# A small early write to the output by every DMA engine, in a batched matrix multiplication that is bound by its transfers

## The chip, the cores and the metric

The kernel runs on one core of one Trainium2 chip. The metric is the time of one execution on the device, in microseconds (us). Where a ratio of two kernels is given, it is the mean time of one kernel's fast runs over that of the other's fast runs of the same rounds, so it isn't quite the ratio of the medians quoted beside it.

## The reference

```python
batch, m, k, n = 16, 512, 512, 512          # float32
def reference(a, b):                        # a: (batch, m, k), b: (batch, n, k)
    return np.matmul(a, b.transpose(0, 2, 1))
```

a, b and out have 16.8 MB each, 50.3 MB in all, and each byte crosses the core's DMA engines once.

## The kernel before

Matrices are worked on in pairs: eight loads of 2 MB from a, eight from b, sixteen stores of 1 MB. VectorE casts to bf16, TensorE transposes and multiplies, VectorE and ScalarE empty PSUM. The first load of b goes through ScalarE's queue, all others through SyncE's; the first eight stores go through GpSimd's queue, the others through SyncE's. The parts that matter here:

```python
        def load(n, engine=nc.sync):
            u, slot = n // 2, n % NL                      # NL = 7 load buffers
            ...
            engine.dma_start(ld[:, slot], src).then_inc(s_ld[slot], 16)

        def store(n):
            engine = nc.gpsimd if n < STORES.count("S") else nc.sync
            engine.wait_ge(s_out, n + 1)
            engine.dma_start(
                out[n].rearrange("(p j) n -> p j n", j=J), ob[:, n % NO]
            ).then_inc(s_st[n], 16)                        # NO = 7 output buffers

        load(0)
        load(1, nc.scalar)
        for n in range(2, NL):
            load(n)
        # ... SyncE: further loads and the late stores ...

        n_st = n_of = 0
        nc.gpsimd.wait_ge(s_ld[0], 32)      # hold the stores until the eighth load has landed
        for what in STORES:                 # "SSSSOSOSOSSOOOOOO": S = store, O = wait for one to land
            ...
```

## Time and profile before

| | |
|---|---|
| time, median of the first three runs | 125.56 us (125.42 to 125.84) |
| span of the profiled run | 123.7 us |
| TensorE, ScalarE, VectorE busy | 73%, 55%, 55% of the span |
| DMA engines busy | nearly all of the span, about 430 GB/s while they are (407 over the whole span) |
| first packet, last landing | 1.93 us, 122.26 us |

How to read it: a busy share is an average over the span, so what counts is which row is full from end to end. Here that is the DMA row. The lines that show it stand in the prediction.

The table by stretches counts a packet's bytes where the packet starts; a packet of 16 KB on 16 engines is 0.26 MB per turn, so in a stretch of 4 us it is a few per cent off. The finer reading takes every packet of the trace, spreads its bytes over its own duration and asks how many microseconds a stretch lost against 430 GB/s. I call that its **deficit**.

### The profile page before, as it was taken

The numbers are of one execution on the slowest core, as the hardware profiler recorded it, in microseconds if no ns is written. First come the engines' busy times: TensorE is split into PE (matmuls) and PEld (weight loads), VectorE is DVE, ScalarE is ACT, GpSimd is POOL, SyncE is SP. The second block draws the span as 40 slices with busy tenths as digits, with TensorE's granted clock in tenths as the row PEclk, the third lists the DMA queues.
The fourth block names the chain that finished last, engine by engine and source line by source line (L and its number), as shares of the span: only waits on it lengthen the run. The fifth ranks groups of instructions, "written<-read, shape, count | busy, mean of one in ns | idle before, by whom it ended". The sixth has DMA issues, their size and how long they took to land. (4 is left out here: it accounts for less than half of the span.)

```text
span 123.7 us, 2364 instructions
## 1 busy us (share of the span) xinstructions
PE 90.8 (73%) x768; PEld 55.9 (45%) x768; DVE 68.1 (55%) x96; ACT 68.0 (55%) x130; POOL 5.2 (4%) x14
## 2 busy tenths in 40 slices
PE   0000189999999899989998999999899919995000
PEld 0000177447644754674476347645754528441000
DVE  0000698983895689289918974865957078400000
ACT  4000065478855956795589369765946069655000
POOL 2000000000000250001010110000000000000000
PEclk9999999999999999999999999999999986999955
DMA  4999999999999999999999999999999999999990
GB/s 148 413 435 429 429 429 424 429 424 435 435 424 424 429 392 363 445 416 424 453 405 437 443 408 443 424 424 458 397 445 427 408 429 427 429 427 429 424 387 8
DMA packets 4608, 50.33 MB, mean 407 GB/s; under 512 B 512, under 2 KB 512, under 8 KB 512
## 3 DMA queue, kind: packets, MB, share of 16 engines
q1 hardware_dynamic: 3312, 39.85, 76.2%
q0 software_dynamic: 1152, 8.39, 16.1%
q10 hardware_dynamic: 144, 2.10, 4.2%
HBM read 33.55 MB, written 16.78 MB: 407 GB/s over the span
## 5 line engine op out<-in xcount | busy, mean ns | idle before, releaser
L249 PE MATMUL ps<-tb,ta 128*128 128x512 bf16 x256 | 57.8, 379 | 0.5
L207 ACT COPY ob<-ps 128x512 f32 x64 | 34.4, 589 | 29.2 <-PE ps L249 21.3
L189 ACT COPY ta<-tp 128x512 bf16<-128x512 bf16 x64 | 32.9, 610 | 15.0 <-PE tp L230 15.0
L249 PEld LDWEIGHTS ps<-tb,ta 128*128 128x128 bf16 x256 | 24.1, 98 | 30.6 <-issue 4.0
L230 PE MATMUL tp<-ident,ha 128*128 128x128 bf16 x256 | 19.3, 228 | 18.1 <-PEq L135 18.1
L230 PEld LDWEIGHTS tp<-ident,ha 128*128 128x128 bf16 x256 | 16.3, 102 | 21.9 <-issue 20.1
L170 DVE COPY tb<-tp 128x1024 bf16<-128x1024 bf16 x32 | 21.2, 684 | 4.2 <-DVEq L135 4.2
L230 PE MATMUL tp<-ident,hb 128*128 128x128 bf16 x256 | 18.5, 230 | 3.4 <-PEq L135 3.4
L230 PEld LDWEIGHTS tp<-ident,hb 128*128 128x128 bf16 x256 | 16.3, 103 | 4.0 <-issue 4.0
L154 DVE CAST ha<-ld 128x1024 bf16 x8 | 5.5, 687 | 14.3 <-DVEq L135 14.3
L165 DVE COPY ha<-wa 128x2048 bf16<-128x2048 bf16 x8 | 5.5, 691 | 12.7 <-DVEq L135 12.7
L160 DVE CAST wa<-ld 128x2048 bf16 x8 | 9.8, 1220 | 0.0
L160 DVE CAST wb<-ld 128x2048 bf16 x8 | 9.7, 1217 | 0.0
L154 DVE CAST hb<-ld 128x1024 bf16 x8 | 5.5, 692 | 7.3 <-DVEq L135 7.3
L103 POOL DMA_DIRECT2D out_dram<-ob x8 | 4.5, 570 | 65.5 <-DMA ld<-in_b_dram 40.9
L169 DVE COPY hb<-wb 128x2048 bf16<-128x2048 bf16 x8 | 5.5, 685 | 0.1
L157 DVE CAST ha<-ld 128x1024 bf16 x8 | 5.5, 686 | 0.0
L157 DVE CAST hb<-ld 128x1024 bf16 x8 | 5.5, 686 | 0.0
L180 ACT ACT_TABLE_LOAD x1 | 1.3, 1283 | 1.5 <-SPq L43 1.5
L79 POOL TENSOR_SCALAR_AFFINE_SELECT ident<-ident 128x128 bf16<-128x128 bf16 x1 | 0.3, 283 | 0.2 <-POOL ident L77 0.2
L77 POOL MEMSET ident<- 128x128 bf16 x1 | 0.2, 204 | 0.5 <-SPq L43 0.5
L180 ACT COPY one<-const-float32-1.0 128x1 f32<-128x1 f32 x1 | 0.2, 192 | 0.0
(4 smaller groups left out, 0.4 us busy)
## 6 DMA issues: line engine op xcount, KB each, us to landing
ld<-in_a_dram SPq DMA_DIRECT2D x8, 2048.0 KB, 26.5
ld<-in_b_dram SPq DMA_DIRECT2D x7, 2048.0 KB, 29.6
out_dram<-ob POOLq DMA_DIRECT2D x8, 1024.0 KB, 28.9
out_dram<-ob SPq DMA_DIRECT2D x8, 1024.0 KB, 19.7
ld<-in_b_dram ACTq DMA_DIRECT2D x1, 2048.0 KB, 12.0
```

The lines of the kernel that those rows point to most:

```text
L103: engine.dma_start(out[n].rearrange("(p j) n -> p j n", j=J), ob[:, n % NO]).then_inc(s_st[n], 16)
L154: nc.vector.tensor_copy(out=h[:, :J, :], in_=src[:, :J, :HK]).then_inc(s_cd, 1)
L157: nc.vector.tensor_copy(out=h[:, J:, :], in_=src[:, J:, :HK]).then_inc(s_c, 1)
L160: nc.vector.tensor_copy(out=w[:], in_=src[:, :, HK:]).then_inc(s_w, 1)
L165: nc.vector.tensor_copy(out=ha[:], in_=wa[:]).then_inc(s_ca, 1)
L169: nc.vector.tensor_copy(out=hb[:], in_=wb[:]).then_inc(s_cb, 1)
L170: nc.vector.tensor_copy(out=tb[:, ko, :], in_=tp[:, 2 + ko % 2].rearrange("k j p -> k (j p)"),).then_inc(s_eb, 1)
L180: nc.scalar.copy(out=one[:], in_=nc.const_aps.tensor(1.0, (P, 1), f32))
L189: c = nc.scalar.copy(out=ta[:, ko, e * J * P:(e + 1) * J * P].rearrange("k (j p h) -> k j p h", j=J, h=2), in_=tp[:, ko % 2, :, e * HP:(e ...
L207: c = nc.scalar.copy(out=dst[:, j, :].rearrange("m (p j) -> m p j", j=2 * J), in_=ps[:, j, :].rearrange("m (j p) -> m p j", j=2 * J),)
L230: t = nc.tensor.transpose(tp[:, 2 * x + g, j, :], h[:, j, g * P:(g + 1) * P], ident[:])
L249: t = nc.tensor.matmul(ps[:, j, :], ta[:, ko, (e * J + j) * P:(e * J + j + 1) * P], tb[:, ko, :].rearrange("k (j p) -> k j p", j=2 * J)[:, ...
```

## The change

Nothing is removed. ScalarE's queue, behind the first load of b, writes one zero by each of the sixteen DMA engines into the first megabyte of out (a "touch"), and GpSimd waits for this ahead of its first store, which later writes the right numbers there. The intent, as far as the edit shows it: let what the first write into out costs be paid early.

```diff
+        s_touch = sem("s_touch")
 ...
         load(0)
         load(1, nc.scalar)
+
+        nc.scalar.dma_start(
+            out[0].rearrange("(i r) n -> i r n", i=16)[:, 0, :1],
+            nc.const_aps.tensor(0.0, (16, 1), f32),
+            allow_slow_non_contiguous=True,
+        ).then_inc(s_touch, 16)
         for n in range(2, NL):
             load(n)
 ...
         n_st = n_of = 0
+        nc.gpsimd.wait_ge(s_touch, 16)
         nc.gpsimd.wait_ge(s_ld[0], 32)
```

## The prediction

> **What bounds the kernel now.** I read the forty-slice view first, then the chain that ended last, then a table of busy time by stretches, then the waits, and last the transfers one by one (start, length, size and queue of each packet, and the moment of each landing).
>
> The page's slices:
>
> ```profile
> PE   0000189999999899989998999999899919995000
> ...
> DMA  4999999999999999999999999999999999999990
> GB/s 148 413 435 429 429 429 424 429 424 435 435 424 424 429 392 363 445 416 424 453 405 437 443 408 443 424 424 458 397 445 427 408 429 427 429 427 429 424 387 8
> DMA packets 4608, 50.33 MB, mean 407 GB/s; under 512 B 512, under 2 KB 512, under 8 KB 512
> ```
>
> A slice is 123.7 / 40 = 3.09 us. The DMA row shows 9 from the second slice to the last but one, so the sixteen engines never rest. TensorE, at 73% of the span, starts in the fifth slice and is done before the stores are. The chain that ended last agrees in an indirect way: it stops at ScalarE's last copy, at 113.08 us, and accounts for only some 10% of the span. What lies after it is stores draining. The last store was issued at 113.7 us, its packets ended at 121.8 us and it landed at 122.26 us, so at the end the engines still had 8 us of queued work that computing could not shorten. **The bound is DMA throughput**: 50.33 MB at 430 GB/s is 117.1 us; the rest is 1.9 us before the first packet, one engine that trails the other fifteen by 1.1 us at the end (122.26 against 121.12 us), 1.4 us of closing, and two soft spots.
>
> The soft spots are what the change can touch. The table by stretches (columns: us from the start, length, busy time of PE, PEld, DVE, ACT, POOL, granted clock, DMA share, GB/s):
>
> ```profile
> 0.00:4.00 4.00, 0.00 (x0) 0.00 (x0) 0.00 (x0) 1.48 (x2) 0.69 (x6) 1.00 0.56 197
> 4.00:12.00 8.00, 0.00 (x0) 0.00 (x0) 0.00 (x0) 0.00 (x0) 0.00 (x0) 1.00 1.00 426
> ...
> 40.00:44.00 4.00, 3.51 (x58) 3.18 (x57) 2.49 (x4) 4.00 (x9) 1.44 (x3) 1.00 1.01 430
> 44.00:48.00 4.00, 3.94 (x27) 1.91 (x25) 3.72 (x6) 2.11 (x6) 0.88 (x2) 1.00 1.00 363
> 48.00:52.00 4.00, 4.00 (x27) 2.02 (x25) 2.25 (x3) 2.71 (x6) 0.00 (x0) 1.00 0.98 414
> 52.00:100.00 48.00, 44.44 (x395) 27.08 (x392) 31.88 (x46) 31.48 (x62) 2.21 (x4) 1.00 1.01 429
> ```
>
> From 44 to 52 us the engines are as busy as ever (share 1.00 and 0.98) and yet move less: 363 and 414 instead of 430. The missing bytes are 4 us x (430 - 363) + 4 us x (430 - 414) = 268 + 64 = 332 kB, which at 430 GB/s is **0.77 us**. In the packets one sees what that is: a load packet of 16 KB takes 611 ns everywhere else, but from 44.37 to 47.2 us each engine has three or four that take 740 to 996 ns, and 57 such packets between 40 and 52 us add up to 0.67 us per engine. The first packet of any store starts at 46.93 us, at the very end of the dip. The waits say what began just before:
>
> ```profile
> POOL out_dram L103 <- DMA ld<-in_b_dram: 40.9, 1, 40.9
> POOL out_dram L103 <- DMA out_dram<-ob: 24.6, 3, 11.0
> ```
>
> GpSimd sat until the eighth load had landed (42.26 us), then issued its first four stores together, at 42.56 to 44.88 us. So the dip goes with the first stores. It doesn't return: between 52 and 100 us two slow packets are to be found, though some seven megabytes of out land in it, and when the stores move to SyncE's queue nothing is lost either. It is a cost paid once, and the change is evidently aimed at it.
>
> **What the Trainium skill says.** "DMA: Bandwidth & Descriptors", section "Issuing engines are not separate DMA queues": transfers from whatever queue run on the same sixteen engines and interleave. The trace agrees: ScalarE's queue (4.2% of the engines' time) and SyncE's first loads together fill the engines (426 GB/s from 4 to 12 us), no more. The touch therefore takes its time from the loads.
> The same page, section "Why a DMA increments its semaphore by 16 and not by 1": the slowest dimension of both sides decides how many engines take part; here it is 16, so sixteen engines write one number each. No run yet shows it.
> The same page, section "Specifications": transfers under 512 B are done by read-modify-write. The trace has no such write of data; its only packets under 512 B are the 512 semaphore increments, of 9 ns each.
> The same page, section "Anatomy of one DMA — SWDGE (gpsimd) path", gives about 2 us of fixed cost, mostly the confirmation of the last write. The trace has less for a store on SyncE's queue: 122.26 - 121.8 = 0.5 us. No page that I found says that an engine's first write, or its first use of a queue, costs extra.
>
> **The change part by part.** Removed: nothing.
> - *One issue on ScalarE's queue.* The issue of the first b load takes 386 ns there; one more puts the table load and the first copy about 0.4 us later, from 1.48 to about 1.9 us. ScalarE's next work comes at about 16 us. Cost on the path: 0.
> - *Sixteen packets of 4 bytes and sixteen semaphore increments*, one pair on each engine, behind b's last packets (11.3 us) and b's increments (12.02 to 12.51 us). At the 9 ns of a 4-byte packet that is 0.02 us per engine; if each held its engine for half a microsecond (the confirmation above), 0.5 us.
> - *Landing of b.* Its increments stand ahead of the touch in the same queue; DVE's start at 13.5 us waits for a and for b, not for the touch. Cost 0, or up to 0.5 us early in the kernel, which matters only as lost DMA time.
> - *GpSimd's wait.* The touch should land at 13 to 15 us; GpSimd is held to 42.26 us anyway. Cost 0.
> - *What moves.* If the dip belongs to the first write into out, that first write is now at 12.5 us. The dip at 44 us goes (-0.77 us), and whatever the write costs is paid at 12.5 us.
>
> The engines have no free time at 12.5 us either (from 12 to 16 us they move 446 GB/s). So moving the cost is worth nothing by itself; only a first write that is cheaper alone than under four stores gains. Nothing stands between the dip and the end but queued transfers, so a gain or a loss in DMA time reaches the end one for one.
>
> **The rivals.**
> 1. *The cost belongs to the first write and shrinks.* For it: a dip at the first stores and at no later ones. The touch writes within the same megabyte as store 0. With 0.77 us gone and 0.1 to 0.3 us paid: about 125.0 us.
> 2. *The cost belongs to the first write and merely moves.* For it: at least fifteen of the sixteen first packets on ScalarE's queue took 787 to 1175 ns instead of 611, so first uses do cost, and the engines are as full at 12.5 us as at 44. About 125.5 us.
> 3. *The cost belongs to the first use of GpSimd's queue, or to four stores being issued in a burst.* For it: the slow packets are loads, ahead of the first store packet, and begin 1.8 us after GpSimd's first issue; stores on SyncE's queue never show it. A touch from ScalarE's queue then changes nothing there: 125.6 us, or 125.8 if the touch itself stalls the engines a little.
> 4. *A partial write is dear:* a stall of 1 us or more at 12.5 us with the dip still there, 126.5 us. Against it: data keeps flowing at 429 GB/s while store increments wait for their confirmations from 52 us on.
>
> I give 0.3, 0.2, 0.43 and 0.07.
>
> **Range and chances.** The mean is 0.3 x 125.0 + 0.2 x 125.5 + 0.43 x 125.65 + 0.07 x 126.5 = 125.5; the best case pulls the middle down slightly, and I say **125.4 us**. The runs of the kernel before spread over 125.42 to 125.84, so about 0.2 us either side is noise. Eight in ten: 124.7 to 126.0, from rival 1 less the noise to rival 3 plus the noise. Two per cent would be 2.5 us; removing the whole dip gives 0.8 us, so faster by more than 2% would need a second effect that I don't see: 0.02. Slower by over 2% would need a stall of over 2.5 us on every engine: 0.02. Within 2%: 0.96.
>
> **What would show it right or wrong.** The touch: sixteen more pairs of small packets on ScalarE's queue, landing before 16 us. The stretch from 44 to 52 us: at 425 or more, rivals 1 or 2; at about 363 and 414, rival 3. The stretch from 12 to 16 us: below 430, the cost has moved there. ScalarE's table load 0.4 us later and nothing else of it changed. GpSimd's first issue still near 42.5 us, released by the eighth load. The last landing should move by just the difference of the two stretches; if it doesn't, the one-for-one step is wrong. The prediction fails if the touch delays a or b by microseconds, or if the one engine that trails by 1.1 us changes its lag.

## The result and the profile after

The changed kernel took 125.53 us (median of 6 runs, 125.43 to 125.70), the kernel before 125.52 us (6 runs, 125.26 to 125.84); ratio 0.9998, 95% interval 0.998 to 1.0016. The change does nothing to the time.

The slices and the queues of the changed kernel's page:

```profile
DMA  4999999999999999999999999999999999999980
GB/s 117 398 440 429 424 435 424 440 440 429 429 424 429 424 413 376 453 411 424 461 395 448 429 413 453 411 419 459 408 445 424 411 432 421 427 424 424 432 379 8
DMA packets 4640, 50.33 MB, mean 407 GB/s; under 512 B 544, under 2 KB 544, under 8 KB 544
...
q10 hardware_dynamic: 176, 2.10, 4.4%
...
out_dram<-const-float32-0.0 ACTq DMA_DIRECT2D x1, 0.1 KB, 12.4
```

The touch is there: 32 more packets than the 4608 of before, all on ScalarE's queue (176 in place of 144), sixteen of them the numbers and sixteen the semaphore increments. The last column of the last line is the time from issue to landing. The packets give its landings as 13.12 to 13.77 us, each 0.61 us behind the same engine's increment for b: one load packet of the other queue comes in between.

The table by stretches of the changed kernel (columns as in the prediction):

```profile
0.00:4.00 4.00, 0.00 (x0) 0.00 (x0) 0.00 (x0) 1.47 (x2) 0.69 (x6) 1.00 0.55 172
4.00:12.00 8.00, 0.00 (x0) 0.00 (x0) 0.00 (x0) 0.00 (x0) 0.00 (x0) 1.00 1.02 434
12.00:16.00 4.00, 0.64 (x7) 0.68 (x8) 2.23 (x3) 0.00 (x0) 0.00 (x0) 1.00 0.99 422
...
44.00:48.00 4.00, 3.94 (x29) 1.94 (x27) 3.59 (x6) 2.18 (x5) 1.39 (x3) 1.00 1.02 399
48.00:52.00 4.00, 4.00 (x24) 2.00 (x23) 2.37 (x4) 2.65 (x5) 0.00 (x0) 1.00 0.98 416
```

Read against the rows of before, this looks like a story. From 44 to 48 us there are 399 GB/s where there were 363: the dip at the first stores seems halved. In the first four microseconds there are 172 where there were 197: the start seems to have become slower by about as much. In deficits: the dip (44 to 52 us) went from 0.71 to 0.37 us, the start (0 to 8 us) from 2.49 to 2.73 us, and the last landing from 122.26 to 122.21 us. A gain of 0.34 and a loss of 0.24 would explain an unchanged time neatly: the touch helps the stores and hurts the start. Two traces, one of each kernel, can't show that, and the first experiment shows that the unchanged kernel has both marks as well, without a touch.

The touch's own passage left no mark: between 12 and 17 us each load packet that started took 611 ns, as elsewhere. GpSimd's waits and first issues:

```profile
POOL out_dram L104 <- DMA ld<-in_b_dram: 41.5, 1, 41.5
...
43.14 2.25 POOL L104 DMA_DIRECT2D out_dram<-ob  x4 [41.46 <-DMA ld<-in_b_dram]
```

It is still the eighth load that lets GpSimd go, at 43.14 in place of 42.56 us, and not the touch.

### The profile page after: what moved, and what is told of

Same layout as the page of the kernel before. It is cut to its first block, busy times and chain, and to the rows that moved or that the text cites. A ratio compares the mean times of both kernels' runs of the same rounds, so it can differ in the third digit from the quotient of the medians.

```text
span 123.6 us, 2365 instructions
## 1 busy us (share of the span) xinstructions
PE 89.4 (72%) x768; PEld 54.4 (44%) x768; DVE 67.9 (55%) x96; ACT 68.0 (55%) x130; POOL 5.3 (4%) x14
## 5 line engine op out<-in xcount | busy, mean ns | idle before, releaser
L238 PE MATMUL tp<-ident,ha 128*128 128x128 bf16 x256 | 18.8, 224 | 19.6 <-PEq L143 19.6
L238 PE MATMUL tp<-ident,hb 128*128 128x128 bf16 x256 | 17.4, 222 | 3.2 <-PEq L143 3.1
L238 PEld LDWEIGHTS tp<-ident,hb 128*128 128x128 bf16 x256 | 15.3, 100 | 3.7 <-issue 3.7
```

The source lines that it names most:

```text
L238: t = nc.tensor.transpose(tp[:, 2 * x + g, j, :], h[:, j, g * P:(g + 1) * P], ident[:])
```

## The experiments

Theory A: the touch takes part of the dip away, and its issue makes the start slower. Theory B: the dip's size is chance, and the touch does nothing at all. Beside that, three theories of the dip itself: the first write into out, the first use of GpSimd's queue, or a burst of four stores.

### The unchanged kernel again, twice

No edit.

> The kernel before, unchanged, for a second trace: how far do the two soft spots vary by themselves? In the first trace the slow 16 KB packets cost 0.39 us per engine in the first 6 us and 0.67 us between 40 and 52 us; in the changed kernel's trace 0.61 and 0.35. Theory (the touch halves the dip at 44 us and slows the start): near 0.39 and 0.67 again. Rival (both numbers are chance from run to run): values as far off as 0.6 and 0.35 turn up here too. Time 125.5 us.

> The kernel before, unchanged, for a third trace: the dip at the first stores was 0.71 us and 0.25 us in the first two. Expected if it is chance: somewhere between 0.1 and 0.8 us, the start (deficit in the first 8 us) between 2.45 and 2.8 us.

Measured: 125.67 and 125.46 us (one run each). The second and the third trace of the kernel before, rows for 0 to 4 and 44 to 52 us:

```profile
0.00:4.00 4.00, 0.00 (x0) 0.00 (x0) 0.00 (x0) 1.47 (x2) 0.69 (x6) 1.00 0.52 168
...
44.00:48.00 4.00, 3.94 (x30) 2.06 (x28) 3.50 (x6) 2.30 (x5) 1.14 (x3) 1.00 1.00 401
48.00:52.00 4.00, 4.00 (x23) 1.88 (x22) 2.50 (x4) 2.52 (x5) 0.00 (x0) 1.00 0.99 422
```

```profile
0.00:4.00 4.00, 0.00 (x0) 0.00 (x0) 0.00 (x0) 1.48 (x2) 0.69 (x6) 1.00 0.55 180
...
44.00:48.00 4.00, 3.94 (x29) 1.94 (x27) 3.60 (x6) 2.17 (x5) 1.06 (x3) 1.00 0.99 379
48.00:52.00 4.00, 4.00 (x25) 2.00 (x24) 2.37 (x4) 2.65 (x5) 0.00 (x0) 1.00 0.96 408
```

The kernel without any touch has a smaller dip in its second trace (401 and 422 GB/s) than the changed kernel had, and an equally slow start (168). Its deficits at the dip are 0.71, 0.25 and 0.49 us in three traces, at the start 2.49, 2.72 and 2.60. The first trace, on which the prediction rests, happened to have the largest dip and the quickest start of the three.

### The changed kernel again

No edit.

> The changed kernel, unchanged, for a second trace and more pairs of runs. Expected: dip at the first stores anywhere in the range that untouched kernels show (0.24 to 0.71 us), time within 0.2 us of the kernel before. If the touch did halve the dip, it should be near 0.37 us again.

Measured: 125.58 us (6 runs; before 125.52 in 11 runs), ratio 1.0006, interval 0.9989 to 1.0024. Deficit at the dip 0.34 us, at the start 2.69 us. The dip is near 0.37 again, which the text had named as a sign for theory A; but it also lies within what the unchanged kernel shows, so this run alone doesn't choose. The table further down puts it beside all the others.

### The touch issued later

```diff
         nc.scalar.copy(out=one[:], in_=nc.const_aps.tensor(1.0, (P, 1), f32))
+        nc.scalar.wait_ge(s_ld[1], 16)
+        nc.scalar.dma_start(  # the same touch, moved here from behind load(1, nc.scalar)
 ...
```

> The same touch, but ScalarE issues it only when b has landed (about 13 us), so that its descriptors are out of the way of the first loads. Theory (touch helps the dip by 0.3 us, its issue hurts the start by 0.2 us): start back at about 0.4 us of excess, dip at about 0.35, time about 125.2 us. Rival (start and dip vary by chance): both as chance has them, time 125.5 us. Rival (a first write costs wherever it is): slow packets at 14 us, time 125.5 us or more.

Measured: 125.57 us (before 125.55), ratio 1.0004, interval 0.9991 to 1.0017. The start is slow (2.80 us) although nothing of the touch is issued before 13.47 us. So its issue isn't what slows the start: theory A loses that half. The dip was 0.13 us, the smallest of all, and yet the time is the same. The touch was issued at 13.47 to 13.83 us and its first write began at 16.92 us.

### The touch in four megabytes

```diff
-            out[0].rearrange("(i r) n -> i r n", i=16)[:, 0, :1],
-            nc.const_aps.tensor(0.0, (16, 1), f32),
+            out[:4].rearrange("e (i r) n -> i e r n", i=16)[:, :, 0, :1],
+            nc.const_aps.tensor(0.0, (16, 4, 1), f32),
```

> The touch as in the change, but in each of the first four megabytes of out (64 numbers): the four stores that are issued together all go to megabytes that have been written. Theory 'first write into each megabyte costs': the dip falls well below the 0.35 us of the changed kernel, to about 0.1 us, time about 125.2 us. Theories 'GpSimd's queue' and 'burst': dip as in the changed kernel or before (0.35 to 0.7 us), time 125.5 us.

Measured: 125.69 us (before 125.55), ratio 1.0008, interval 0.9995 to 1.0021. The deficit at the dip is 0.57 us. All four megabytes that the first stores write had been written before, so a first write by small numbers into a megabyte doesn't prepay the dip.

### GpSimd's queue used early, by a load and by a write

```diff
+        nc.gpsimd.dma_start(                      # gp_load; behind the identity matrix
+            few[:], a[0].rearrange("(i r) k -> i r k", i=16)[:, 0, :1],
 ...
+        ).then_inc(s_touch, 16)                   # in both runs ScalarE's touch is taken out
```

```diff
+        nc.gpsimd.dma_start(                      # gp_touch
+            out[0].rearrange("(i r) n -> i r n", i=16)[:, 0, :1],
+            nc.const_aps.tensor(0.0, (16, 1), f32),
 ...
+        ).then_inc(s_touch, 16)
```

> No touch of out: instead GpSimd's own queue is used once early, for a load of 16 numbers from a into a spare tile, and GpSimd waits for it ahead of the first store. Theory 'first use of GpSimd's queue' : the dip between 44 and 52 us goes (excess under 0.15 us per engine), time about 124.9 to 125.2 us. Theory 'first write into out': dip stays at 0.6 us, time 125.5 us. Theory 'burst of four stores': dip stays at 0.35 to 0.7 us, time 125.5 us.

> The touch issued from GpSimd's own queue in the first microseconds: both the first use of the queue that the stores use and the first write into out are over before 12 us. Theory 'either of the two causes the dip, and only both together take it away': dip under 0.1 us between 44 and 52 us. Rival 'the dip comes with real stores beginning beside loads, and its size is chance (0.13 to 0.71 us in six traces so far)': a dip within that range. Time 125.3 to 125.7 us in both.

Measured: the load 125.48 us (before 125.55), ratio 0.9999, interval 0.9985 to 1.0013; the write 125.53 us (before 125.48), ratio 1.0004, interval 0.9987 to 1.002. Deficits at the dip 0.24 and 0.46 us. With the write, every engine has used the queue that the stores use, and written into the first megabyte of out, before 9 us, and the dip is there:

```profile
44.00:48.00 4.00, 3.75 (x39) 2.32 (x37) 3.50 (x6) 2.71 (x6) 1.72 (x4) 1.00 0.98 373
48.00:52.00 4.00, 4.00 (x20) 1.81 (x19) 3.62 (x5) 2.72 (x6) 0.00 (x0) 1.00 1.00 424
```

Both theories, first use of the queue and first write into out, fall, as far as small transfers can stand for them.

### All traces side by side

Deficits in us against 430 GB/s, from the packets of each trace whose first stores come at 42 to 44 us:

| kernel | start, 0 to 8 us | dip, 44 to 52 us |
|---|---|---|
| before, three traces | 2.49, 2.72, 2.60 | 0.71, 0.25, 0.49 |
| changed, two traces | 2.73, 2.69 | 0.37, 0.34 |
| touch later | 2.80 | 0.13 |
| touch in four megabytes | 2.79 | 0.57 |
| GpSimd's queue: load, write | 2.77, 2.62 | 0.24, 0.46 |
| 32 numbers by each engine (below) | 2.71 | 0.22 |

The kernels with some write into out ahead of the stores have dips of 0.13 to 0.57 us, those without one (before, and the GpSimd load) 0.24 to 0.71 us. The ranges overlap nearly wholly. A slow start tends to go with a small dip (the correlation over these ten traces is -0.7), so the sum of the two varies less (2.93 to 3.36 us) than either; why, these runs don't tell.

### Without the hold, and with a longer one

```diff
-        nc.gpsimd.wait_ge(s_ld[0], 32)            # no_hold: removed
+        nc.gpsimd.wait_ge(s_ld[1], 32)            # hold_more: s_ld[1] in place of s_ld[0]
```

> The kernel before without GpSimd's wait for the eighth load: stores are issued singly as their results are ready, from about 25 us on, so no burst of four at 42 us. Theory 'the dip belongs to the first stores, whatever queue or count': a dip of 0.1 to 0.7 us at about 27 to 32 us, none at 44 us, time 125.3 to 125.7 us. Theory 'a burst of four stores causes it': no dip anywhere, time about 125.1 us. Theory 'each time stores begin beside loads': several dips, time 126 us or more.

> The kernel before with the stores held until the ninth rather than the eighth load from the queue's start has landed (about 47 us, 5 us later). Theory 'the dip goes with the first stores': it moves to 49 to 53 us, and 44 to 48 us runs at 429 GB/s. Rival 'something else at 44 us slows the loads': the dip stays at 44 to 48 us. Time 125.5 us, since the same bytes move.

Measured: without the hold 126.27 us (before 125.48), ratio 1.0057, interval 1.0035 to 1.008; with the longer one 125.92 us, ratio 1.0036, interval 1.0019 to 1.0053. Both moved the dip. Without the hold, stores are issued singly, the first at 28.01 us, the next two at 30.19 and 39.51:

```profile
28.00:30.00 2.00, 2.00 (x26) 1.46 (x24) 0.00 (x0) 1.40 (x4) 0.67 (x1) 1.00 1.06 451
30.00:33.00 3.00, 2.50 (x43) 2.22 (x41) 2.49 (x4) 3.00 (x7) 0.82 (x1) 1.00 0.95 333
33.00:38.00 5.00, 4.94 (x30) 2.30 (x28) 4.81 (x8) 3.06 (x6) 0.00 (x0) 1.00 1.03 439
...
44.00:48.00 4.00, 3.94 (x32) 2.13 (x30) 3.50 (x6) 2.47 (x5) 0.00 (x0) 1.00 1.06 451
...
110.00:120.00 10.00, 7.90 (x47) 3.63 (x44) 1.32 (x3) 5.56 (x11) 0.00 (x0) 1.00 0.82 343
```

The dip lies at 30 to 33 us (0.50 us between 29 and 33 us), and there is none at 44. With the longer hold GpSimd's first issue was at 47.83 us:

```profile
44.00:48.00 4.00, 3.94 (x32) 2.12 (x30) 3.50 (x6) 2.46 (x5) 0.17 (x1) 1.00 1.03 438
48.00:52.00 4.00, 4.00 (x21) 1.82 (x19) 2.75 (x4) 2.37 (x5) 2.87 (x4) 1.00 1.03 393
52.00:56.00 4.00, 3.51 (x60) 3.22 (x59) 2.49 (x4) 4.00 (x9) 0.00 (x0) 1.00 0.94 399
```

The stretch from 48 to 54 us lost 0.48 us while that from 40 to 48 us lost 0.03. So the dip goes with the first stores, wherever they are. It needs no burst: in the run without the hold, the slow packets began at 30.0 us, when a single store stood in the queue, and the single early store of the next run paid 0.41 us.

The time of the run without the hold was mis-expected (126.27 in place of 125.3 to 125.7 us). The last row of that run shows why: near the end the engines were busy for only 0.82 of the time. With the stores taking bandwidth early, the loads come later (the last one landed at 102.19 us, before at 99.49), and the computing that waits for it no longer hides behind queued stores. The hold earns 0.8 us here. The longer hold's 0.4 us stays unexplained: the run that was profiled was its fastest (125.64 us), and its trace doesn't show it.

### A whole store early

```diff
+        nc.gpsimd.wait_ge(s_ld[2], 16)
+        nc.gpsimd.dma_start(
+            out[0].rearrange("(p j) n -> p j n", j=J), ld[:, 2, :J, :]
+        ).then_inc(s_touch, 16)
+        nc.gpsimd.wait_ge(s_touch, 16)
 ...                                               # in load(n), before the third buffer is loaded anew:
+            if n == NL + 2:
+                nc.sync.wait_ge(s_touch, 16)
```

> A whole early store in place of the touch: at about 18 us GpSimd sends one megabyte of loaded data to the first megabyte of out (wrong numbers, which store 0 overwrites later), and waits for it; nothing else goes through its queue until 42 us. Theory 'the dip is paid each time stores begin to run beside loads': a dip at about 19 to 23 us and another one of 0.13 to 0.71 us at 44 to 48 us. Rival 'paid once, by the first full-size writes': a dip at about 19 to 23 us and none (under 0.08 us) at 44 to 52 us. Time: one megabyte more at 430 GB/s is 2.4 us, so about 128.0 us in both.

Measured: 128.20 us (before 125.52), ratio 1.0221, interval 1.019 to 1.0252. The megabyte costs its 2.4 us. The stretches of this kernel:

```profile
16.00:20.00 4.00, 3.52 (x34) 3.17 (x33) 4.00 (x6) 2.05 (x4) 0.91 (x1) 1.00 1.01 434
20.00:24.00 4.00, 3.94 (x40) 2.67 (x39) 3.46 (x7) 2.12 (x5) 0.00 (x0) 1.00 0.95 360
24.00:28.00 4.00, 4.00 (x20) 1.86 (x19) 3.93 (x5) 2.73 (x6) 0.00 (x0) 1.00 1.04 442
```

The early store paid the dip: 0.41 us between 20 and 24 us. Its packets ran from 23.0 to 30.5 us, and from then on loads had the engines alone until the four stores, issued at 46.09 us, began to run at 50 us. There the deficit is 0.09 us (49 to 52 us; 0.08 over the 44 to 52 us of the table), less than in any other trace's dip but not nothing. One trace can't tell 0.09 from the smallest dip seen (0.13), so "paid once, by the first full-size writes" is the better supported of the two theories and isn't settled. Either way, prepaying gained nothing: the cost was only paid earlier.

### The touch made larger

```diff
-            out[0].rearrange("(i r) n -> i r n", i=16)[:, 0, :1],
-            nc.const_aps.tensor(0.0, (16, 1), f32),
+            out[0].rearrange("(i r) (c d) -> i (r c) d", i=16, c=4)[:, :, :1],   # many_touch
+            nc.const_aps.tensor(0.0, (16, 128, 1), f32),
```

```diff
+            out[0].rearrange("(i r) n -> i r n", i=16)[:, :, :1],                # touch_32
+            nc.const_aps.tensor(0.0, (16, 32, 1), f32),
```

> The touch made 128 times larger: 128 numbers by each engine (2048 separate 4-byte writes) into the first megabyte of out, on ScalarE's queue behind b as in the change. It measures the touch's own cost, which the change is too small to show. Theory (a 4-byte write costs its engine about 9 ns, like a semaphore increment): 128 x 9 ns = 1.2 us lost between 12 and 20 us, time about 126.7 us. Rival (the time that the profile gives a small write isn't its whole cost; partial writes stall the engine): tens of us. Rival (small writes fit into gaps): 125.5 us. If the lost DMA time and the longer run agree, the step that DMA time reaches the end one for one is shown too.

> 32 numbers by each engine instead of 1 or 128. In the run with 128 the small writes took turns with load packets, one for one, so they ended at 82 us, GpSimd's wait for them held the first store until 82.5 us, and the run took 18.4 us more. Theory 'that was GpSimd's wait alone; a small write costs its engine 9 ns': with 32 the touch is over at about 12 + 32 x 0.62 = 32 us, ahead of 42 us, so the first store is issued near 42.5 us as before and the time is 125.5 + 0.3 = 125.8 us. Rival '0.145 us of engine time per small write': 125.5 + 4.5 = 130 us.

Measured with 128 numbers by each engine: 143.90 us (before 125.48), ratio 1.1459, interval 1.144 to 1.1478, far from the 126.7 us expected. The waits and two of the page's rows:

```profile
POOL out_dram L104 <- DMA out_dram<-const-float32-0.0: 80.9, 1, 80.9
```

```profile
PE   0000599989999998993000000599989989989920
...
DMA  4999999999999999999999749999996490291094
```

The small writes of an engine took turns with its load packets, nearly one for one: from 12.3 to 81.7 us in the packets, 0.54 us per write, or some 1.1 writes to a load packet of 611 ns. Until then GpSimd waited (80.9 us), no store was issued, the seven output buffers filled, ScalarE stopped, TensorE stopped (six empty slices), and at last the loads ran out as well (the DMA row falls to 7 and 4). The 18.4 us are nearly all GpSimd's wait, as the run with 32 numbers shows, in which the eighth load and not the touch let GpSimd go:

```profile
POOL out_dram L104 <- DMA ld<-in_b_dram: 41.7, 1, 41.7
```

Its small writes end at 31.4 us, ahead of the eighth load, the first store is issued at 43.36 us, and the time is 125.66 us (before 125.52), ratio 1.0008, interval 0.9988 to 1.0027. By the finer reading the engines moved 426.9 GB/s from 14 to 30 us there, against 430.9 in the changed kernel; that is 16 us x 4.0 / 430.9 = 0.15 us for 29 small writes per engine, 5 ns each (128 of them would be 0.7 us of the 18.4). So the one write per engine of the change costs next to nothing, and the wait costs nothing as long as the touch lands ahead of 42 us.

## Why the prediction was right

The time, 125.53 us, is within 0.13 us of the one forecast, and within the range. That by itself says little of the mechanism: only some 0.8 us was at stake, three of the four rivals lay between 125.0 and 125.65 us, and the noise is 0.2 us, so the range would have held with any of these three. As to the cause of the dip, the right number was partly luck. Step by step:

- **The bound** was read rightly. Every kernel that moved these bytes with full engines to the end took 125.5 to 126 us, whatever its stores' queue was used for before.
- **The touch's own cost** of 0.02 us per engine holds as an upper value: 5 ns per write by the run with 32 numbers, and load packets of 611 ns while it passed. The other term, half a microsecond per engine if each held its engine until its write was confirmed, falls with the same run.
- **GpSimd's wait costs 0**: shown, with its limit. In the run with 128 numbers the very same wait was nearly the whole of 18.4 us.
- **ScalarE's table load** came 0.5 us later (1.98 in place of 1.48 us), 0.4 expected; nothing waited for it. The two signs that would have made the prediction fail didn't come: DVE started at 13.77 us (13.50 to 13.75 in the three traces of before), and the last engine trailed by 1.25 us (1.14 to 1.49).
- **"It is a cost paid once"**: that the dip belongs to the first stores and doesn't come back holds but for remains of 0.07 to 0.30 us in the 48 us from 52 to 100 us, in the ten traces of the table (with 32 numbers they are more than the dip, 0.30 against 0.22). But its **size** was taken from one trace, and that step failed: 0.77 us there (0.71 by the finer reading), 0.25 and 0.49 us in two more traces of the same kernel. A reading of the packets was off too: from 44.37 to 47.2 us there are 44 slow packets over sixteen engines, so two or three on most of them, not three or four.
- **One for one to the end**: the two traces agree as far as they go (dip -0.34, start +0.24, last landing -0.05 us), and the early megabyte of 2.4 us came out as 128.20 - 125.52 = 2.7 us. But where the engines rest near the end, as without the hold, the step doesn't hold.
- **The rivals.** Rivals 1 and 2 had the cost belong to the first write into out, and small writes there didn't take it away. With a full-size write rival 2 comes nearest to what was seen: the early store moved the dip to 20 to 24 us (0.41 us) and left 0.08 us. Rival 3, the likeliest, gave the right time for two reasons, and neither was borne out: neither an early small use of GpSimd's queue nor the absence of a burst took the dip away. Its remark that stores on SyncE's queue never show the dip is no evidence, since they are issued from 73 us on, long after the first stores. Rival 4 is ruled out by the run with 32 numbers.
- **The signs to look for** were too coarse. A dip "at 425 or more" against "363 and 414" can't be judged from one trace each, and 422 GB/s from 12 to 16 us, below 430, would by its wording have shown that the cost had moved there, while the packets in that stretch were as fast as ever.

What stays open: what makes loads slow while the first full-size stores make their way into the engines, why the size of the dip varies, and whether one full-size packet by each engine would prepay it. In every run the first full-size stores went through GpSimd's queue; whether the dip belongs to full-size work on that queue or to full-size stores on any queue was not tried. A small effect of the touch on the dip (the mean without a write ahead of the stores is 0.42 us in four traces, with one 0.35 in six) can be neither shown nor excluded by these traces; the times exclude one beyond 0.2% of the run.

## What to carry to other kernels

Before explaining a difference of half a microsecond between two traces, trace the unchanged kernel again: here the traces of the unchanged kernel differed at the dip by up to 0.46 us, those of the two kernels first compared by 0.34. Where the DMA engines are full from end to end, moving a transfer cost to an earlier time gained nothing here; it would have to shrink, or move to where the engines are idle (which no run here tried). Many tiny writes cost an engine little (5 ns each here), but nearly each took its turn behind a large packet of the other queue, so don't let anything wait for the last of them.

## What the Trainium skill lacked or had wrong

- "DMA: Bandwidth & Descriptors", section "Latency and other measured facts", gives about 0.6 us to the first byte for the queues of SyncE and ScalarE and about 1 us for GpSimd's. Behind idle engines GpSimd's figure is about right (with 128 numbers the first store was issued at 82.54 and its first packet began at 83.78 us, 1.2 us), while ScalarE's first load took 1.0 us from its issue (0.91 to 1.93 us). Beside a full queue both are too low: 42.56 to 46.93 us for the first store, 1.92 to 5.74 us for the early load of 16 numbers, 13.47 to 16.92 us for the later touch, so 3.4 to 4.4 us. The page has no figure for that.
- The same page, section "Queues, rings and completion order", says that an engine turns between queues packet by packet, a packet being typically 9 to 17 descriptors. The turning is seen, but here nearly every 4-byte write took a turn of its own (some 1.1 to a load packet): 128 of them took 69 us beside loads.
- No page says that loads run slower while the first full-size stores (here on GpSimd's queue) make their way in: 0.13 to 0.71 us per engine in ten traces, up to 996 ns per 16 KB packet in place of 611 in the first, over about 3 us.
